# Moving the right operands of four matmul groups by 32 to 192 bytes, with pads in the on-chip memory

## The chip, the cores and the metric

The kernel runs on one core of a Trainium2 chip. The metric is the device time of one execution in microseconds (us), of which the median over several executions is taken. Lower is better.

## The reference

One decoder block for 512 tokens of width 1024, all in float32:

```
h = rmsnorm(x, pre_mix_norm)
q_r, k_r, v_r, g_r, q_s, k_s, v_s, gate_r, gate_s = split(h @ w_in)
y_r = (silu(g_r) * retention(q_r, k_r, v_r)) @ w_ret_out      # 4 heads, chunks of 128
y_s = sliding_window_attention(q_s, k_s, v_s, sinks) @ w_swa_out  # 8 heads, window 128
x = x + rmsnorm((sigmoid(gate_r) * y_r + sigmoid(gate_s) * y_s) @ w_out, post_mix_norm)
u = square(relu(rmsnorm(x, pre_mlp_norm) @ w_up))             # width 4096
out = x + rmsnorm(u @ w_down, post_mlp_norm)
```

## The kernel before

Every large product is made of three matmuls: each float32 operand is split in a high and a low part (`split`, lines 133 to 136: ScalarE casts the high part at L135, VectorE subtracts it at L136), and `mm3` (L176 to 181) adds high x high (L179), high x low (L180) and low x high (L181) in PSUM. A matmul holds one operand, the left one, still in the array (128 x 128, brought there by a weight load, PEld in the profile) and streams the other, the right one (256 or 512 columns), past it. TensorE (PE) loads the left operand of the next matmul while it streams the right one of the present matmul, so two reads of the on-chip memory run side by side.

The stages, in order of time, with the names that the profile gives to output, right and left operand:

- **Projections** (0 to 206 us): `ptok` (keys and values of the attention; right operand `wkv`, left `xg`), `pblk` (queries and keys; right `xg`, later `hT`; left `whi` and `wlo`, the split weights), `wide` (a fast matrix multiplication with seven products for v and g; here the weights stream, and `hT` and `hsum` are the left operands), with the attention and the retention between them.
- **Output of attention and gates** (206 to 354 us): `ys`, then eight calls of `wino_pair` (seven products of 256 columns instead of eight; right operands `hT` and the sums of its quarters `hsum`; left `whi`, `wlo` and the prepared sums `p24`, `p22`, which the profile calls `p`), between which `yr` (right `retT`) runs.
- **Mixing** (354 to 400 us): `ps` (left `mhi` and `mlo`, right `wo`).
- **Up projection** (400 to 557 us): `up` for three weight pairs (right `h2c`, `h2b`, `h2d`), then thirteen calls of `wino_pair` (right `h2c`, `h2d` and the sums `h2s`).
- **Down projection** (557 to 720 us): seven products with 512 columns, `p1` to `p7` (the profile calls them `p`), whose left operands are split from the activations `uc` by `left` (L1139) into the tiles `left0` and `left1`, and whose right operands are split from the weights (`raw`, `tch`). The last quarter runs in two halves of 256 columns, `p4c`.

Tiles lie in pools that are stacked one behind the other in each partition; when a pool is closed, later pools take its memory. A `pad` is a tile that nobody uses; it shifts what is allocated behind it:

```
def pad(pool, size, name="pad"):

    pool.tile([P, size // 4], F32, name=name, bufs=1)
```

All the tiles of a matmul are whole multiples of 256 bytes long, so that a tile's start modulo 256 is set by the pads ahead of it. The split weights `whi`, `wlo`, the sums `p24`, `p22`, and the tiles `xg`, `retT`, `swaT`, `mhi`, `wo` and `left` start at 128 modulo 256 in the built program. `hT`, `hsum`, `wkv`, `h2c`, `h2b`, `h2d` and `h2s` start at 64. The distance of this document is the start of the left operand less the start of the right one, modulo 256: 64 for `pblk` and `wino` with `hT` and `hsum`, for `ptok`, and for everything with `h2...`; 192 for `wide`; 0 for `ys`, `yr`, `ps`, `p`, `p4c`, the part of `pblk` with `xg`, and the products of the retention (`ret_st`, `ret_v`).

The order of the instructions is made by a scheduling layer: it places an instruction on its engine as soon as the tiles that it reads and writes allow, with priorities that the code gives (`high_priority`, `issue_after`). Where a new tile takes bytes of a closed pool's tile, the new tile's writer waits for the last reader of the old one. That matters between up and down projection: the pool `ring` with `left0` and `left1` (L1139) takes memory of `uctx`, which holds `h2c`, `h2d`, `h2s`, `p24`, `p22`. In the built program `h2s` ends at byte 141,888 of a partition, and the first `left0` begins at 141,952.

Of the kernel before, what the change touches and what calls it, by code (L numbers as in the profile page):

```python
# [94 lines left out]
def block_kernel(ctx, tc, x, xT, pre_mix, w_in, w_v, w_g, w_gate, w_ret, w_swa, w_out, sinks, post_mix,  # L95
# [13 lines left out]
    def pad(pool, size, name="pad"):  # L109

        pool.tile([P, size // 4], F32, name=name, bufs=1)
# [29 lines left out]
    def parts(src, shape):  # L141
        hi = stream.tile(shape, F32R, name="whi", tag="whi")
        lo = stream.tile(shape, F32R, name="wlo", tag="wlo")
        split(hi, lo, src)
        return hi, lo
# [149 lines left out]
    accpool = ctx.enter_context(tc.tile_pool(name="accpool", bufs=1))  # L295
    hctx = ExitStack()
    hpool = hctx.enter_context(tc.tile_pool(name="hpool", bufs=1))
    pad(hpool, 192)
    hT = [hpool.tile([P, KD, SEQ], F32R, name=f"hT{i}") for i in range(2)]
    hsum = [hpool.tile([P, 4, 4, 256], F32R, name=f"hsum{i}") for i in range(2)]  # L300


# [210 lines left out]
    def ret_keys(kT, h):  # L513

        ps = bank([P, NT - 1, P], "ret_k")
        for c in range(NT - 1):
            nc.tensor.transpose(ps[:, c, :], kT[:, c * P : (c + 1) * P], ident)
        kd = [rpool.tile([P, NT - 1, P], F32R, name=f"kd{i}", bufs=1) for i in range(2)]
        scale = chunk_sb[:, 0, h : h + 1]
        nc.scalar.mul(kd[0], ps, scale)  # L520
        nc.vector.scalar_tensor_tensor(
            kd[1], ps, scale, f(kd[0]), op0=ALU.mult, op1=ALU.subtract
        )
        return kd

    def ret_scores(qT, kT, h):
        ps = bank([P, NT, P], "ret_s")
        for c in range(NT):
            sl = slice(c * P, (c + 1) * P)
            nc.tensor.matmul(ps[:, c, :], kT[:, sl], qT[:, sl], start=True, stop=True)  # L530
        p = rpool.tile([P, NT, P], F32, name="pt", tag="qk")
        pt = [rpool.tile([P, NT, P], F32R, name=f"pt{i}", bufs=1) for i in range(2)]
        nc.vector.tensor_tensor(
            p, ps, decay_sb[:, h : h + 1, :].to_broadcast([P, NT, P]), op=ALU.mult
        )
        split(pt[0], pt[1], p)
        return pt
# [61 lines left out]
    def wide_sums(pool, w_, **kw):  # L599

        both = pool.tile([P, 2, 4, 512], F32, name="acc", **kw)
        sx, sy = both[:, 0], both[:, 1]
        nc.sync.dma_start(sx, w_[1, 0])
        nc.gpsimd.dma_start(sx, w_[1, 1], accum_op=ALU.add)
        nc.sync.dma_start(sy, w_[0, 0])
        return sx, sy
# [64 lines left out]
    def load_qk(h):  # L671
        return load_feature_blocks(w_in, (C_QR + h * RET_DK, C_KR + h * RET_DK))
# [67 lines left out]
    for h in range(RET_HEADS):  # L740
        if 0 < h < RET_HEADS - 1:
            wqk = load_qk(h + 1)
        v = parts(vg[:, :, h * RET_DV : (h + 1) * RET_DV], [P, NT, RET_DV])
        if h == RET_HEADS - 1:
            vg = vpool.tile([P, NT, D_MODEL], F32, name="vg", tag="vg")
            steps = wide(w_g, *wide_sums(xypool, w_g), vg)
            next(steps)
        kd = ret_keys(kT, h)
        pt = ret_scores(qT, kT, h)
        q_now = qc  # L750
        if h + 1 < RET_HEADS:
            qT = ret_block(wqk[0])
        else:
            next(steps)
        if h == 0:
            probs_t = swa_transpose(probs)
        states = ret_states(kd, v, h)
        if h == 0:
            swa_values(3, probs_t)

            bctx.close()
            gctx = ExitStack()
            wx = wino_pool(gctx)
            pad(wx, 64)
            xyctx = ExitStack()
            xypool = xyctx.enter_context(tc.tile_pool(name="xypool", bufs=1))
        if h + 1 < RET_HEADS:
            kT = ret_block(wqk[1])
        else:
            next(steps)  # L770
        ret_values(q_now, pt, states, v, h)
        if h + 1 < RET_HEADS:
            qc = [rpool.tile([P, SEQ - P], F32R, name=f"qc{i}", bufs=1) for i in range(2)]
            split(qc[0], qc[1], qT[:, P:])
# [226 lines left out]
    uctx = ExitStack()  # L1001
    h2pool = uctx.enter_context(tc.tile_pool(name="h2pool", bufs=1))
    h2spool = uctx.enter_context(tc.tile_pool(name="h2spool", bufs=1))
    pad(h2pool, 192)
    h2c = [h2pool.tile([P, 2, 4, 256], F32R, name=f"h2c{i}") for i in range(2)]
    h2d = [h2spool.tile([P, 4, 256], F32R, name=f"h2d{i}") for i in range(2)]
    h2s = [h2spool.tile([P, 4, 4, 256], F32R, name=f"h2s{i}") for i in range(2)]
    rspool = uctx.enter_context(tc.tile_pool(name="rspool", bufs=1))
    px = uctx.enter_context(tc.tile_pool(name="px", bufs=1))
    pad(px, 64)  # L1010
    wx = wino_pool(uctx)
    pctx = ExitStack()
    ppool = pctx.enter_context(tc.tile_pool(name="ppool", bufs=1))
    pad(ppool, 192)
    h2b = [ppool.tile([P, 4, 256], F32R, name=f"h2b{i}") for i in range(2)]
    quads = [
        [tuple(a[:, 0] for a in h2c), tuple(h2b)],
# [348 lines left out]
```

## Time and profile before

| | us |
|---|---|
| median of 3 runs | 724.63 (721.85 to 732.5) |
| span of the profiled execution | 719.9 |
| median less span | 4.7 |
| PE busy | 708.3 (98% of the span) |
| VectorE (DVE) busy | 535.8 (74%) |
| ScalarE (ACT) busy | 421.7 (59%) |
| GpSimd (POOL) busy | 60.3 (8%) |
| mean granted TensorE clock | 0.999 of full speed |

The span runs from the first to the last instruction of the one execution that was profiled; what lies around it is the difference to the runs' times. A matmul's duration holds a constant latency besides its streaming: matmuls of 256 columns that follow each other at 0.11 us each show 276 ns. So durations of different groups are compared among those of the same column count, and only what one has more than another costs time. In the view of one tile, a row gives the smallest, the median and the largest duration of a group, and when its first and last instruction started.

### The profile page before, as it was taken

What the parts mean: (1) busy time and instruction counts of PE and PEld (TensorE: products, weight loads), DVE (VectorE), ACT (ScalarE), POOL (GpSimd) and SP (SyncE); (2) the same over time, 40 slices, a digit from 0 to 9 for tenths busy, and PEclk for the clock granted to TensorE, in tenths of its full rate; (3) what the DMA queues carried; (4) which work ended last, traced back from release to release, by engine and by line L of the source; (5) the groups of instructions that cost most, each with busy time, mean ns of one, the idle gap of its engine ahead of it and who ended that gap; (6) DMA issues with size and microseconds to landing.
All of it is one profiled execution on the core that took longest, in us unless ns stands there. A gap on an engine that the chain in (4) does not pass through costs nothing.

```text
span 719.9 us, 11248 instructions
## 1 busy us (share of the span) xinstructions
PE 708.3 (98%) x4438; PEld 628.8 (87%) x4438; DVE 535.8 (74%) x808; ACT 421.7 (59%) x712; POOL 60.3 (8%) x75
## 2 busy tenths in 40 slices
PE   8999999999999999999999999999999999999996
PEld 7877878888888989989888999999999888888885
DVE  5699986667885667566845876877776788977797
ACT  6667676345665526344643776666668666655571
POOL 0200000201100000000002100000000110010010
PEclk9999999999999999999999999999999999999999
DMA  9964424916444455461563618777753999698603
GB/s 318 330 179 84 108 72 129 282 46 132 101 142 120 107 162 147 125 197 59 198 271 117 159 47 234 201 202 193 204 153 118 305 278 238 151 208 194 118 0 117
DMA packets 43605, 117.79 MB, mean 164 GB/s; under 512 B 3488, under 2 KB 21024, under 8 KB 37408
## 3 DMA queue, kind: packets, MB, share of 16 engines
q1 hardware_dynamic: 36784, 80.76, 31.8%
q0 software_dynamic: 6480, 36.18, 27.3%
q8 instruction: 35, 0.57, 0.3%
q14 instruction: 18, 0.15, 0.1%
q10 hardware_dynamic: 288, 0.14, 0.1%
HBM read 114.96 MB, written 2.10 MB: 163 GB/s over the span
## 4 chain that ended last, share of the span: by engine, by line
PE 79%; DVE 8%; DMA 5%; ACT 4%; issue 2%; POOL 0%; POOLq 0%; DVEq 0%; SPq 0%; ACTq 0%
PE wino L179 9%; PE wino L180 9%; PE wino L181 9%; PE p L181 5%; PE p L180 5%; PE p L179 5%; DVE wlo L136 3%; PE wide L179 3%; PE wide L180 3%; PE wide L181 3%; DMA raw<-in_w_in 3%; PE ps L180 2%; PE ps L181 2%; PE yr L181 2%; PE yr L180 2%; PE yr L179 2%
## 5 line engine op out<-in xcount | busy, mean ns | idle before, releaser
L136 DVE TENSOR_TENSOR wlo<-raw,whi 128x1024 fp32r<-128x1024 f32 x81 | 98.6, 1223 | 42.4 <-ACT whi L135 42.2
L135 ACT CAST whi<-raw 128x1024 fp32r<-128x1024 f32 x81 | 84.8, 1052 | 40.4 <-DMA raw<-in_w_down 7.6
L181 PE MATMUL p<-whi,left 128*128 128x512 f32 x216 | 84.1, 390 | 0.2 <-DVE left L136 0.2
L180 PE MATMUL p<-wlo,left 128*128 128x512 f32 x216 | 84.2, 390 | 0.0
L179 PE MATMUL p<-whi,left 128*128 128x512 f32 x216 | 84.0, 390 | 0.1
L181 PEld LDWEIGHTS p<-whi,left 128*128 128x128 f32 x216 | 40.5, 188 | 9.3 <-DVE left L136 1.0
L180 PEld LDWEIGHTS p<-wlo,left 128*128 128x128 f32 x216 | 40.5, 188 | 8.9 <-DVE wlo L136 0.4
L179 PEld LDWEIGHTS p<-whi,left 128*128 128x128 f32 x216 | 40.5, 188 | 8.7 <-ACT left L135 0.5
L136 DVE TENSOR_TENSOR wlo<-tch,whi 128x1024 fp32r<-128x1024 f32 x32 | 38.6, 1220 | 6.9 <-ACT whi L135 6.9
L135 ACT CAST left<-uc 128x1024 fp32r<-128x1024 f32 x28 | 29.3, 1050 | 23.4 <-PE p L180 23.4
L135 ACT CAST p<-rs 128x1024 fp32r<-128x1024 f32 x21 | 22.1, 1051 | 35.5 <-DVE rs L230 35.4
L136 DVE TENSOR_TENSOR left<-uc,left 128x1024 fp32r<-128x1024 f32 x28 | 34.1, 1221 | 10.4 <-ACT left L135 10.4
L135 ACT CAST whi<-tch 128x1024 fp32r<-128x1024 f32 x32 | 33.2, 1050 | 11.3 <-PE p L181 6.8
L136 DVE TENSOR_TENSOR p<-rs,p 128x1024 fp32r<-128x1024 f32 x21 | 25.7, 1226 | 15.4 <-ACT p L135 15.4
L136 DVE TENSOR_TENSOR wlo<-rs,whi 128x1024 fp32r<-128x1024 f32 x21 | 25.7, 1224 | 12.1 <-ACT whi L135 9.4
L136 DVE TENSOR_TENSOR wlo<-acc,whi 128x1024 fp32r<-128x1024 f32 x20 | 24.1, 1217 | 6.5 <-ACT whi L135 6.5
L179 PE MATMUL wino<-h2s,p 128*128 128x256 f32 x104 | 28.7, 276 | 0.0
L180 PE MATMUL wino<-h2s,p 128*128 128x256 f32 x104 | 28.7, 276 | 0.0
L181 PE MATMUL wino<-h2s,p 128*128 128x256 f32 x104 | 28.7, 276 | 0.0
L179 PE MATMUL wino<-h2c,whi 128*128 128x256 f32 x104 | 28.7, 276 | 0.0
L180 PE MATMUL wino<-h2c,whi 128*128 128x256 f32 x104 | 28.7, 276 | 0.0
L181 PE MATMUL wino<-h2c,wlo 128*128 128x256 f32 x104 | 28.7, 276 | 0.0
(354 smaller groups left out, 2317.7 us busy)
## 6 DMA issues: line engine op xcount, KB each, us to landing
tch<-in_w_down POOLq DMA_DIRECT2D x12, 1024.0 KB, 9.5
raw<-in_w_down SPq DMA_DIRECT2D x7, 1024.0 KB, 7.6
rs<-in_w_up SPq DMA_DIRECT2D x13, 512.0 KB, 4.2
rs<-in_w_up POOLq DMA_DIRECT2D x13, 512.0 KB, 5.7
raw<-in_w_up SPq DMA_DIRECT2D x13, 512.0 KB, 5.1
raw<-in_w_in SPq DMA_DIRECT2D x8, 512.0 KB, 5.2
acc<-in_w_v POOLq DMA_DIRECT2D x4, 1024.0 KB, 7.9
rs<-in_w_gate SPq DMA_DIRECT2D x8, 512.0 KB, 3.9
```

Source lines behind the costliest of these rows:

```text
L135: last["hi"] = nc.scalar.copy(hi, src)
L136: last["split"] = nc.vector.tensor_tensor(lo, src, f(hi), op=ALU.subtract)
L179: nc.tensor.matmul(ps, ah, bh, start=first, stop=False, skip_group_check=more)
L180: nc.tensor.matmul(ps, ah, bl, start=False, stop=False, skip_group_check=more)
L181: nc.tensor.matmul(ps, al, bh, start=False, stop=last, skip_group_check=more)
```

## The change

Six pads change their size or are new. No instruction is added or taken away. The diff in full:

```
-    pad(hpool, 192)
+    pad(hpool, 224)
     hT = [hpool.tile([P, KD, SEQ], F32R, name=f"hT{i}") for i in range(2)]
+    pad(hpool, 64, "pad2")
     hsum = [hpool.tile([P, 4, 4, 256], F32R, name=f"hsum{i}") for i in range(2)]
...
             wx = wino_pool(gctx)
-            pad(wx, 64)
+            pad(wx, 224)
             xyctx = ExitStack()
...
-    pad(h2pool, 192)
+    pad(h2pool, 160)
     h2c = [h2pool.tile([P, 2, 4, 256], F32R, name=f"h2c{i}") for i in range(2)]
+    pad(h2spool, 64, "pad2")
     h2d = [h2spool.tile([P, 4, 256], F32R, name=f"h2d{i}") for i in range(2)]
+    pad(h2spool, 160, "pad3")
     h2s = [h2spool.tile([P, 4, 4, 256], F32R, name=f"h2s{i}") for i in range(2)]
     rspool = uctx.enter_context(tc.tile_pool(name="rspool", bufs=1))
     px = uctx.enter_context(tc.tile_pool(name="px", bufs=1))
-    pad(px, 64)
+    pad(px, 128)
     wx = wino_pool(uctx)
     pctx = ExitStack()
     ppool = pctx.enter_context(tc.tile_pool(name="ppool", bufs=1))
-    pad(ppool, 192)
+    pad(ppool, 224)
     h2b = [ppool.tile([P, 4, 256], F32R, name=f"h2b{i}") for i in range(2)]
```

In the built program the tiles then start as follows (modulo 256), and the left operands `whi`, `wlo`, `p24`, `p22`, `xg` stay at 128:

| matmuls (count) | columns | moved tile | start before, now | distance before, now |
|---|---|---|---|---|
| `pblk` with `hT` (192) | 512 | `hT`, right | 64, 96 | 64, 32 |
| `wide` with `hsum` (192) | 512 | `hsum`, left | 64, 160 | 192, 32 |
| `wide` with `hT` (144) | 512 | `hT`, left | 64, 96 | 192, 224 |
| `wino` with `hT`, gates (288) | 256 | `hT`, right | 64, 96 | 64, 32 |
| `wino` with `hsum`, gates (384) | 256 | `hsum`, right | 64, 160 | 64, 224 |
| `ptok` (96) | 256 | `wkv`, right | 64, 160 | 64, 224 |
| `up` and `wino` with `h2c` (456) | 256 | `h2c`, right | 64, 32 | 64, 96 |
| `up` and `wino` with `h2d`, `h2b` (300) | 256 | `h2d`, `h2b`, right | 64, 96 | 64, 32 |
| `wino` with `h2s` (624) | 256 | `h2s`, right | 64, 0 | 64, 128 |

`h2s` now ends at byte 142,080, and the first `left0` still begins at 141,952: the two share 128 bytes. That moves instructions between up and down projection. On ScalarE at that place, before (in the rows, `left` is `left0`, `raw` and `tch` hold weights of the down projection, `uc` the activations):

```order
L276 COPY uc_3640<-wino 128x256
L135 CAST whi<-tch_4440 128x1024 x2
L135 CAST left_6073<-uc_3963 128x1024
L135 CAST left_6110<-uc_3963 128x1024
L135 CAST whi<-raw 128x1024 x2
L283 COPY uc_3640<-wino 128x256
L1112 ACTIVATE uc_3640<-wino 128x256
```

With the change:

```order
L276 COPY uc_3641<-wino 128x256
L135 CAST whi<-tch_4443 128x1024 x2
L135 CAST whi<-raw 128x1024
L283 COPY uc_3641<-wino 128x256
L135 CAST whi<-raw 128x1024
L135 CAST left_6076<-uc_3964 128x1024
L135 CAST left_6113<-uc_3964 128x1024
```

The two casts of `left0` have moved behind both casts of `raw`, and the first of them now waits for the last matmul of the last `wino_pair`. On PE at the same place, before (`p_6067` and `p_6068` are `p1`, `left_6073` is the first `left0` and `left_6074` the first `left1`, `p_5924` is `p22`):

```order
L179 MATMUL p_6067<-whi,left_6073 128x512
L180 MATMUL p_6067<-wlo,left_6073 128x512
L179 MATMUL p_6068<-whi,left_6073 128x512
L181 MATMUL p_6067<-whi,left_6074 128x512
...
L179 MATMUL p_6068<-whi,left_6073 128x512
L179 MATMUL wino<-h2s_3976,p_5924 128x256
L180 MATMUL wino<-h2s_3977,p_5924 128x256
...
L180 MATMUL p_6068<-wlo,left_6073 128x512
```

With the change (`p_6070` and `p_6071` are `p1`, `p_6072` and `p_6073` are `p2`):

```order
L181 MATMUL wino<-h2s_3979,p_5928 128x256
L179 MATMUL p_6070<-whi,left_6076 128x512
L180 MATMUL p_6070<-wlo,left_6076 128x512
L179 MATMUL p_6071<-whi,left_6076 128x512
L180 MATMUL p_6071<-wlo,left_6076 128x512
L179 MATMUL p_6072<-whi,left_6113 128x512
L180 MATMUL p_6072<-wlo,left_6113 128x512
L179 MATMUL p_6073<-whi,left_6113 128x512
L181 MATMUL p_6070<-whi,left_6077 128x512
```

Before, ten matmuls of `p1` stood ahead of the last product of the last `wino_pair` (twelve matmuls); now all twelve stand ahead of the first matmul of `p1`, and three of `p2` have moved up between those of `p1`. The load of the weights `tch1` (L1089 before) waits for the end of that last product in both programs.

More of the change, by code (lines that the diff above doesn't have):

```diff
@@ L297, in block_kernel @@
     hpool = hctx.enter_context(tc.tile_pool(name="hpool", bufs=1))
-    pad(hpool, 192)
+    pad(hpool, 224)
     hT = [hpool.tile([P, KD, SEQ], F32R, name=f"hT{i}") for i in range(2)]
+    pad(hpool, 64, "pad2")
     hsum = [hpool.tile([P, 4, 4, 256], F32R, name=f"hsum{i}") for i in range(2)]
@@ L763, in block_kernel @@
             wx = wino_pool(gctx)
-            pad(wx, 64)
+            pad(wx, 224)
             xyctx = ExitStack()
@@ L1003, in block_kernel @@
     h2spool = uctx.enter_context(tc.tile_pool(name="h2spool", bufs=1))
-    pad(h2pool, 192)
+    pad(h2pool, 160)
     h2c = [h2pool.tile([P, 2, 4, 256], F32R, name=f"h2c{i}") for i in range(2)]
+    pad(h2spool, 64, "pad2")
     h2d = [h2spool.tile([P, 4, 256], F32R, name=f"h2d{i}") for i in range(2)]
+    pad(h2spool, 160, "pad3")
     h2s = [h2spool.tile([P, 4, 4, 256], F32R, name=f"h2s{i}") for i in range(2)]
@@ L1009, in block_kernel @@
     px = uctx.enter_context(tc.tile_pool(name="px", bufs=1))
-    pad(px, 64)
+    pad(px, 128)
     wx = wino_pool(uctx)
@@ L1013, in block_kernel @@
     ppool = pctx.enter_context(tc.tile_pool(name="ppool", bufs=1))
-    pad(ppool, 192)
+    pad(ppool, 224)
     h2b = [ppool.tile([P, 4, 256], F32R, name=f"h2b{i}") for i in range(2)]
```

## The prediction

> **What bounds the kernel now.** I read the page first: busy times, granted clock, the chain that ended last.
>
> ```profile
> PE 708.3 (98%) x4438; PEld 628.8 (87%) x4438; DVE 535.8 (74%) x808; ACT 421.7 (59%) x712; POOL 60.3 (8%) x75
> PEclk9999999999999999999999999999999999999999
> PE 79%; DVE 8%; DMA 5%; ACT 4%; issue 2%; POOL 0%; POOLq 0%; DVEq 0%; SPq 0%; ACTq 0%
> ```
>
> PE is busy for 98% of the span, at full clock throughout, and holds 79% of the chain. The view of PE's waits, of which these are the longest and the last row of eight, sums to under 5 us:
>
> ```profile
> PE warm L336 <- POOL ident masks.py:199: 1.4, 1, 1.4
> PE p L181 <- DVE left L136: 0.2, 1, 0.2
> ```
>
> So the time is the number of matmuls by the spacing at which they follow each other. The change leaves the number alone and shifts where operands start; what it can do is change the spacing, or the waits. The next view asks whether spacing differs today among groups of equal shape: one tile's rows, smallest, median and largest duration, first the groups of 256 columns.
>
> ```profile
> L179 PE MATMUL ptok<-wkv,xg x32: 276/276/384, 6.0 to 17.0; 128*128 128x256 f32 x32
> L179 PE MATMUL ret_v<-st,qc x12: 283/283/287, 129.5 to 178.8; 128*128 128x256 f32 x12
> L180 PE MATMUL wino<-hT,whi x64: 276/281/283, 232.3 to 336.4; 128*128 128x256 f32 x64
> L180 PE MATMUL wino<-hsum,p x64: 276/281/281, 235.0 to 343.5; 128*128 128x256 f32 x64
> L179 PE MATMUL up<-h2c,whi x48: 276/281/281, 399.9 to 418.4; 128*128 128x256 f32 x48
> L179 PE MATMUL wino<-h2c,whi x104: 276/276/276, 435.0 to 551.6; 128*128 128x256 f32 x104
> L179 PE MATMUL wino<-h2s,p x104: 276/276/281, 437.7 to 561.2; 128*128 128x256 f32 x104
> L180 PE MATMUL p4c<-wlo,left x16: 280/283/283, 707.2 to 712.6; 128*128 128x256 f32 x16
> ```
>
> Three levels stand there. At distance 0 (`ret_v`, `p4c`) nearly all take 283 ns, 7 more than the floor of 276. At distance 64 there are two levels, 276 and 281: the up projection sits at 276, the gates mostly at 281. The groups of 512 columns:
>
> ```profile
> L179 PE MATMUL pblk<-hT,whi x64: 392/394/496, 42.0 to 160.1; 128*128 128x512 f32 x64
> L179 PE MATMUL pblk<-xg,whi x32: 389/389/501, 17.4 to 41.3; 128*128 128x512 f32 x32
> L181 PE MATMUL wide<-whi,hsum x64: 388/392/397, 61.3 to 201.1; 128*128 128x512 f32 x64
> L181 PE MATMUL wide<-whi,hT x48: 388/394/397, 55.8 to 206.6; 128*128 128x512 f32 x48
> L179 PE MATMUL yr<-retT,whi x64: 389/389/389, 251.7 to 353.9; 128*128 128x512 f32 x64
> L180 PE MATMUL p<-wlo,left x216: 388/389/498, 557.7 to 706.7; 128*128 128x512 f32 x108
> ```
>
> Here distance 0 (`yr`, `p`, `pblk` with `xg`) is the floor, 389, distance 64 (`pblk` with `hT`) takes 394, and 192 (`wide`) lies between, 388 to 397. So the distance goes with the spacing, but not alone: the same distance is good for one column count and bad for the other, and at 64 one group has both levels. The timeline of PE shows where the gates change from one to the other:
>
> ```profile
> 249.62 0.28 PE L180 MATMUL wino<-hsum,whi 128*128 128x256 f32 x1
> 249.73 0.28 PE L181 MATMUL wino<-hsum,wlo 128*128 128x256 f32 x1
> 250.23 0.39 PE L179 MATMUL wino<-hsum,p 128*128 128x256 f32 x1 [0.22 <-ACT sgs L283]
> 250.92 0.28 PE L181 MATMUL wino<-hsum,p 128*128 128x256 f32 x1
> 251.04 0.28 PE L179 MATMUL wino<-hsum,p 128*128 128x256 f32 x1
> 251.16 0.28 PE L180 MATMUL wino<-hsum,p 128*128 128x256 f32 x1
> ```
>
> Ahead of the wait they start every 0.11 us, behind it every 0.12. The view of `wino` for the next stretch of 168 matmuls, first and last row, has no other level any more:
>
> ```profile
> L179 PE MATMUL wino<-hT,whi x16: 281/281/281, 262.6 to 275.0; 128*128 128x256 f32 x16
> L181 PE MATMUL wino<-hsum,p x16: 281/281/281, 265.7 to 282.3; 128*128 128x256 f32 x16
> ```
>
> 167 steps in 19.7 us are 0.118 us each. A short wait thus set a phase between streaming and weight loads that lasted until the gates ended. My theory: the two reads meet in the same part of the memory when their distance, less their lag, falls in a window, and the meeting costs 5 to 7 ns per matmul. [...]
>
> **What could be gained at most.** With the floor of 276 and 389, the moved groups lose: `pblk` with `hT` 192 x 5 ns = 1.0 us; `wide` 336 x 3 (median about 392) = 1.0; the gates 672, three quarters of them at 281, so 672 x 3.8 = 2.6; `up` with `h2c` about half of 144 at 281 = 0.4. Together 5.0 us, 0.7% of the time. The groups that stay at distance 0 keep their 7 ns or nothing, since neither operand moves.
>
> **The terms by group.** No run before has the distances 32, 96, 128 or 224, so each is bounded by the nearest rows: for 256 columns 0 (+7 ns) and 64 (0 or +5), for 512 columns 0 (0), 64 (+5) and 192 (+3). Each term is the count by (chosen less present level); the ends stand in brackets.
>
> - `pblk` with `hT`, 32, between +0 and +5, middle 2.5: 192 x -2.5 ns = -0.5 us (-1.0 to 0).
> - `wide`, 32 and 224, between +0 and +5, middle 2.5, now 3: 336 x -0.5 = -0.2 (-1.0 to +0.7).
> - gates with `hT`, 32, between +0 and +7, middle 3.5, now 3.8: 288 x -0.3 = -0.1 (-1.1 to +0.9).
> - gates with `hsum`, 224: the same ends, as it lies as near to 0: 384 x -0.3 = -0.1 (-1.5 to +1.2).
> - `ptok`, 224, now at the floor: 96 x 3.5 = +0.3 (0 to +0.7).
> - `h2d` and `h2b`, 32, now at the floor: 300 x 3.5 = +1.0 (0 to +2.1).
> - `h2c`, 96: nearest to 64, so I keep its mix with a little on top, 1.0 after 0.8: +0.1 (-0.4 to +2.8).
> - `h2s`, 128: the farthest from 0, where the loss is largest, and 64 beside it is at the floor; I take 0.5 ns: 624 x 0.5 = +0.3 (0 to +4.3).
>
> Sum +0.8 us (-5.0 to +12.7).
>
> [...]
>
> **The moved instructions.** Between up and down projection `left0` now waits for the last reader of `h2s`. Before:
>
> ```profile
> 557.43 0.39 PE L179 MATMUL p<-whi,left 128*128 128x512 f32 x1
> 557.89 0.40 PE L179 MATMUL p<-whi,left 128*128 128x512 f32 x1
> 558.45 0.50 PE L181 MATMUL p<-whi,left 128*128 128x512 f32 x1 [0.16 <-DVE left L136]
> 558.79 0.40 PE L179 MATMUL p<-whi,left 128*128 128x512 f32 x1
> 561.45 0.28 PE L181 MATMUL wino<-h2s,p 128*128 128x256 f32 x1
> ...
> 556.67 1.04 ACT L135 CAST left<-uc 128x1024 fp32r<-128x1024 f32 x1
> 561.77 0.38 ACT L1112 ACTIVATE uc<-wino 128x256 f32<-128x256 f32 x1 [1.89 <-PE wino L181]
> 568.17 2.95 ACT L135 CAST whi<-tch 128x1024 fp32r<-128x1024 f32 x3 [2.29 <-DMA tch<-in_w_down]
> ...
> 570.18 0.39 PE L179 MATMUL p<-whi,left 128*128 128x512 f32 x1
> 570.53 0.19 PEld L180 LDWEIGHTS p<-wlo,left 128*128 128x128 f32 x1 [0.39 <-DVE wlo L136]
> 570.54 0.50 PE L180 MATMUL p<-wlo,left 128*128 128x512 f32 x1
> ```
>
> At a spacing of 0.23, PE lost 0.33 us from 557.89 to 558.45 and 0.11 to 558.79, on `left1`; and 0.13 from 570.18 to 570.54 with another 0.10 behind it, since the weights `tch1` came late. Together 0.67. With the change the twelve matmuls of the last product take the place of the first of `p1` at 557.43, and the next would start at 557.43 + 12 x 0.113 (the 0.118 of the slow gates less 5 ns) = 558.79. The last of them ends 0.28 after its start at 558.68, at 558.96; ScalarE follows 0.04 later (561.45 + 0.28 = 561.73 to 561.77), casts 1.04 and is done at 560.04; with some 0.15 to PE, `p1` starts at about 560.2: 1.4 lost. A new start costs 0.1 more (as at 558.79), and `p2` waits some 0.1 for the second cast: 1.6 in all. Behind the casts, ScalarE's work on `uc` for the third quarter waits, and nobody needs that within 10 us. The load of `tch1` is released at 558.96 in place of 561.73, so its cast comes some 2.8 earlier than 568.17, ahead of its use after 48 matmuls, and the 0.23 there is gone. Net 1.6 - 0.67 = +0.9; I take +1.0 (0 if other work fills the gap, +1.5 if VectorE delays `left1` once more).
>
> **The sum.** 719.9 + 0.8 + 1.0 = 721.7 us of span. The median of the runs lies 4.7 above the span of the profiled execution; kept, that gives 726.4.
>
> **The rivals.**
>
> 1. *All four distances clear the window.* For it: the present levels at 64 and 192 are not far from their floor, and 96 and 128 lie far from 0. Against it: 32 and 224 are the neighbours of 0, which costs 7 ns in every stretch of 256 columns. It would give back the 5.0: 719.9 - 5.0 + 1.0, with 4.7 on top 720.6.
> 2. *The up projection loses its floor: slower.* The place is 411 to 557 us, where today everything runs at 276. If `h2s`, `h2c`, `h2d` and `h2b` go to the 283 of distance 0, 1380 x 7 ns = 9.7 us, less the 0.4 that `h2c` loses now, with the gap of 1.0: 719.9 + 10.3 + 4.7 = 734.9. It decides once the median of `h2s` is above 279. For it: a change of phase by one wait took the gates from 276 to 281, and the up projection holds most of the moved matmuls. Against it: more than 1000 matmuls in a row held the floor.
> 3. *The distance is no cause, and the phase alone sets the level.* Then the pads do not do what they say: each stretch keeps the row it has, and only the moved instructions count: 719.9 + 1.0 + 4.7 = 725.6. For it: both levels at one distance. Against it: 283 at distance 0 in every stretch. [...]
>
> **How the numbers follow.** My forecast, 726.4, has a chance of 0.43, rival 1 0.21, rival 2 0.18, rival 3 0.15; 0.03 is left for levels that no row shows. The sum of the ends is 719.9 - 5.0 + 0 + 4.7 = 719.6 and 719.9 + 12.7 + 1.5 + 4.7 = 738.8. All ends of one sign together are unlikely above; I cut at rival 2 and give 719.5 to 735. About 2%, 14.5 us, is what a measurement of this kernel can tell from no change, since its own runs spread from 721.85 to 732.5. No case here reaches it: faster by over 2% 0.02, within 2% 0.94, slower by over 2% 0.04.
>
> **What would show it.** Right if `pblk` with `hT` falls below 394, `h2d` rises above 276, `h2s` stays within 2 ns of 276, and PE stands still for 1.2 to 1.8 us near the first `p1`. Rows of 276 and 389 everywhere would mean rival 1, a median of 280 or more on `h2s` rival 2, unchanged rows rival 3. A level above 283, or a wait that moves work outside of that one place, would make the working wrong.

## The result, and the profile after

| | before | changed |
|---|---|---|
| median of 18 runs each (us) | 727.02 (721.11 to 736.04) | 731.45 (730.57 to 732.34) |
| ratio of the two, 95% interval | | 1.0083 (1.0062 to 1.0103) |
| span of the profiled execution (us) | 719.9 | 729.9 |

The changed kernel is slower by 0.8%: a real difference, and within the 2% that count as no change. The number lies in the range, 5.0 above the forecast. What happened is not the likeliest case but the second rival: the up projection lost its floor. That rival left out the projections ahead of it, which lost 2 us more.

One thing about the runs of before has to be known to read every comparison below. They lie at two levels: of the 18, five lie between 721.1 and 721.9, nine between 726.3 and 728.5, one at 724.63; three above 732 are disturbed and count in no comparison. The changed kernel has one level, 1.8 us wide. So the change costs 10 us against the lower level, to which the profiled execution belongs (span 719.9), and 4 against the upper one, and the ratio mixes the two. What the two levels are is what experiments 7 to 11 ask.

The page of the changed kernel, total busy time and the engines' shares of the chain:

```profile
span 729.9 us, 11248 instructions
PE 718.0 (98%) x4438; PEld 638.3 (87%) x4438; DVE 535.3 (73%) x808; ACT 422.7 (58%) x712; POOL 63.7 (9%) x75
PE 87%; DVE 5%; DMA 3%; ACT 2%; issue 2%; POOL 0%; DVEq 0%; POOLq 0%; SPq 0%; ACTq 0%
```

The same 4438 records of matmuls take 718.0 us in place of 708.3: PE is as busy as before, and slower in what it does. The groups of 256 columns, in the order in which the prediction shows them (smallest, median, largest duration; first and last start):

```profile
L179 PE MATMUL ptok<-wkv,xg x32: 278/278/420, 6.0 to 19.0; 128*128 128x256 f32 x32
L179 PE MATMUL ret_v<-st,qc x12: 283/283/283, 129.4 to 178.8; 128*128 128x256 f32 x12
L180 PE MATMUL wino<-hT,whi x64: 277/280/285, 232.6 to 338.1; 128*128 128x256 f32 x64
L180 PE MATMUL wino<-hsum,p x64: 277/280/282, 235.5 to 345.2; 128*128 128x256 f32 x64
L179 PE MATMUL up<-h2c,whi x48: 277/281/284, 401.6 to 420.4; 128*128 128x256 f32 x48
L179 PE MATMUL wino<-h2c,whi x104: 277/281/283, 437.8 to 560.2; 128*128 128x256 f32 x104
L179 PE MATMUL wino<-h2s,p x104: 276/283/287, 440.6 to 567.3; 128*128 128x256 f32 x104
L179 PE MATMUL wino<-h2d,p x52: 278/281/285, 442.0 to 563.0; 128*128 128x256 f32 x52
L180 PE MATMUL p4c<-wlo,left x16: 282/283/283, 717.2 to 722.6; 128*128 128x256 f32 x16
```

From 400 us on, where `wino` with `h2c` stood at 276/276/276, no row of the up projection has its median under 280 any more, and most rows of `h2s` are at 283. The groups that did not move (`ret_v`, `p4c`) are where they were. The groups of 512 columns:

```profile
L179 PE MATMUL pblk<-hT,whi x64: 392/396/503, 42.9 to 160.0; 128*128 128x512 f32 x64
L179 PE MATMUL pblk<-xg,whi x32: 387/389/479, 19.3 to 42.3; 128*128 128x512 f32 x32
L181 PE MATMUL wide<-whi,hsum x64: 389/395/397, 62.1 to 201.4; 128*128 128x512 f32 x64
L179 PE MATMUL wide<-whi,hT x48: 392/396/508, 55.9 to 206.5; 128*128 128x512 f32 x48
L179 PE MATMUL yr<-retT,whi x64: 389/389/399, 252.8 to 355.6; 128*128 128x512 f32 x64
L180 PE MATMUL p<-wlo,left x216: 388/389/397, 569.3 to 716.7; 128*128 128x512 f32 x108
```

`pblk` at 32 is as bad as it was at 64. Of the 336 matmuls of `wide`, 99 took 390 ns or less before; 5 do now. The place between up and down projection, on PE and on ScalarE:

```profile
567.56 0.28 PE L181 MATMUL wino<-h2s,p 128*128 128x256 f32 x1
568.97 0.50 PE L179 MATMUL p<-whi,left 128*128 128x512 f32 x1 [1.14 <-ACT left L135]
569.31 0.39 PE L180 MATMUL p<-wlo,left 128*128 128x512 f32 x1
```

```profile
566.32 1.05 ACT L135 CAST whi<-raw 128x1024 fp32r<-128x1024 f32 x1 [0.69 <-PE wino L180]
567.87 1.99 ACT L135 CAST left<-uc 128x1024 fp32r<-128x1024 f32 x2 [0.50 <-PE wino L181]
```

From 567.56 to 568.97 are 1.41 us, 0.11 of which the matmul itself would take: 1.30 lost, for the reason that the prediction worked out and close to its size (1.4).

The sum can be made from the starts of the matmuls. From the start of one to the start of the next, the floor is 113.3 ns for 256 columns and 226.7 for 512 (in the profile of before, the steps of `wino` from 440 to 555 us and the usual steps of `p` from 600 to 700); what a matmul has above it (steps more than 15 ns above are waits and left out) is its group's loss:

| group (distance before, now) | mean loss before, ns | now, ns | change in the sum, us | term of the prediction |
|---|---|---|---|---|
| `pblk` with `hT` (64, 32) | 6.7 | 6.5 | 0.0 | -0.5 |
| `wide` (192; 32 and 224) | 2.6 | 6.5 | +1.3 | -0.2 |
| gates, `hT` and `hsum` (64; 32 and 224) | 3.4 | 4.9 and 3.5 | +0.4 | -0.2 |
| `ptok` (64, 224) | 0.0 | 4.4 | +0.3 | +0.3 |
| `h2d`, `h2b` (64, 32) | near 0 | 5.0 | +1.5 | +1.0 |
| `h2c` (64, 96) | 0.8 | 5.3 | +2.0 | +0.1 |
| `h2s` (64, 128) | 0.05 | 6.0 | +3.7 | +0.3 |

That is 9.2 of the 10.0 us by which the spans differ. The moved instructions are 1.0 more: 1.30 ahead of `p1`, 0.11 behind its first matmul and 0.2 at 580.3 us, where a `left` of VectorE comes late, together 1.64, less the 0.68 that `left1` and the late weights cost there before. Groups that were not moved add 0.2. Waits at the start, in the attention and in the gates differ by up to 1.5 us either way between the two profiles and sum to -0.4.

### The profile page after: what moved, and what is told of

Its sections match the earlier page's. It is cut to its first block, busy times and chain, and to the rows that moved or that the text cites. A ratio compares the mean times of both kernels' runs of the same rounds, so it can differ in the third digit from the quotient of the medians.

```text
span 729.9 us, 11248 instructions
## 1 busy us (share of the span) xinstructions
PE 718.0 (98%) x4438; PEld 638.3 (87%) x4438; DVE 535.3 (73%) x808; ACT 422.7 (58%) x712; POOL 63.7 (9%) x75
## 4 chain that ended last, share of the span: by engine, by line
PE 87%; DVE 5%; DMA 3%; ACT 2%; issue 2%; POOL 0%; DVEq 0%; POOLq 0%; SPq 0%; ACTq 0%
PE wino L179 8%; PE wino L180 8%; PE wino L181 8%; PE p L179 5%; PE p L181 5%; PE p L180 5%; PE wide L179 3%; PE wide L180 3%; PE wide L181 3%; PE pblk L179 3%; PE pblk L181 3%; PE pblk L180 3%; PE yr L179 2%; PE yr L180 2%; PE ps L179 2%; PE ps L180 2%
## 5 line engine op out<-in xcount | busy, mean ns | idle before, releaser
L179 PEld LDWEIGHTS p<-whi,left 128*128 128x128 f32 x216 | 40.5, 188 | 10.3 <-ACT left L135 2.0
L135 ACT CAST p<-rs 128x1024 fp32r<-128x1024 f32 x21 | 22.0, 1050 | 31.3 <-DVE rs L230 31.3
L181 PE MATMUL wino<-h2s,wlo 128*128 128x256 f32 x104 | 29.6, 284 | 0.0
L180 PE MATMUL wino<-h2s,whi 128*128 128x256 f32 x104 | 29.5, 284 | 0.0
L179 PE MATMUL wino<-h2s,whi 128*128 128x256 f32 x104 | 29.5, 284 | 0.0
L180 PE MATMUL wino<-h2s,p 128*128 128x256 f32 x104 | 29.4, 283 | 0.0
L179 PE MATMUL wino<-h2s,p 128*128 128x256 f32 x104 | 29.4, 283 | 0.0
L181 PE MATMUL wino<-h2s,p 128*128 128x256 f32 x104 | 29.3, 282 | 0.0
L179 PE MATMUL wino<-h2c,whi 128*128 128x256 f32 x104 | 29.2, 281 | 0.0
```

Of the source, the lines that this page charges most:

```text
L135: last["hi"] = nc.scalar.copy(hi, src)
L179: nc.tensor.matmul(ps, ah, bh, start=first, stop=False, skip_group_check=more)
L180: nc.tensor.matmul(ps, ah, bl, start=False, stop=False, skip_group_check=more)
L181: nc.tensor.matmul(ps, al, bh, start=False, stop=last, skip_group_check=more)
```

## The experiments

Three theories stood after the result. *Distance*: each group pays for its own distance, as in the table. *Order*: the loss comes from the moved instructions, which also move waits. *Phase*: a wait sets by lot whether a stretch of matmuls runs at its floor or above it, and the pads only changed the lot. Each experiment is the kernel before or the changed one with a short edit.

**1. The changed kernel with the old order.** The pool between `uctx` and the left operands gets 256 bytes more, so that `left0` no longer shares bytes with `h2s`; the distances stay those of the change.

```
-    pad(junks, 256)
+    pad(junks, 512)
```

> The changed kernel with 256 bytes more ahead of the left operands of the down projection, so that they no longer share bytes with h2s; all distances stay those of the change and p1 stands ahead of the last product again, as before. Theory 'distance' (the spacing is set by the distance of left and right operand): the median durations stay at 283 (h2s), 281 (h2c, h2d), 394 to 396 (pblk with hT, wide), the stall of 1.3 us ahead of the first p1 goes, span about 729, 1 us under the changed kernel's 729.9. Theory 'order' (the moved instructions are the loss): the up projection returns to 276 and the span to about 720.

Median 729.68 (10 runs), ratio to before 1.0068 (1.0041 to 1.0095), span 727.4. The wait ahead of `p1` is gone, the levels are not:

```profile
L179 PE MATMUL wino<-h2s,p x104: 276/282/287, 439.7 to 568.9; 128*128 128x256 f32 x104
```

`h2s` loses 6.0 ns per matmul, `h2c` 5.3, `h2d` 5.0, `pblk` and `wide` 6.5, as in the changed kernel. The order is worth 1.3 us by the starts of the matmuls there and 1.8 by the medians, and is not the cause of the rest.

**2. The projections alone.** The pads of `hpool` and of the first `wx` as in the change; `h2c`, `h2b`, `h2d`, `h2s` stay at 64.

```
-    pad(hpool, 192)
+    pad(hpool, 224)
...
+    pad(hpool, 64, "pad2")
...
-            pad(wx, 64)
+            pad(wx, 224)
```

> The kernel before with the new pads of hT and hsum alone; h2c, h2d, h2b, h2s stay at distance 64. Theory 'distance': pblk with hT and wide at 394 to 396, gates at 279 to 281, so up to 1.5 us more than before there; the up projection at 276 or at 281 throughout, by the phase that the last wait leaves (span about 721 or 727). Theory 'start' (an odd multiple of 32 bytes as start of any operand is slow): the same for these groups, and the up projection at 276.

Median 728.14, ratio 1.0031 (0.9995 to 1.0066), span 722.0. `pblk` and `wide` lose 6.5 ns, the gates 4.9 and 3.5, as in the changed kernel, and the up projection stands where it was before:

```profile
L181 PE MATMUL wide<-whi,hsum x64: 389/395/398, 62.2 to 202.5; 128*128 128x512 f32 x64
L179 PE MATMUL wino<-h2s,p x104: 276/276/279, 439.7 to 563.1; 128*128 128x256 f32 x104
```

So this part of the change is worth 2 us, and most of the loss lies behind 400 us. The runs of this kernel, in which only the up projection is still at 64, lie at two levels too: three at 723.3 to 723.8, seven from 727.5 up.

**3. The late `left0` alone.** The kernel before with 256 bytes more ahead of `h2c`: no distance changes, but all of `uctx` ends 256 bytes later.

```
-    pad(h2pool, 192)
+    pad(h2pool, 448)
```

> The kernel before with the pad ahead of h2c at 448 instead of 192 bytes: every distance stays at 64, but h2s now shares bytes with the first left operand of the down projection, so that p1 comes behind the last product as in the changed kernel. Theory 'distance': a stall of 1.3 us ahead of the first p1, 0.7 us of stalls there gone, so 0.5 to 1.0 us more than the kernel before at the same phase; up projection at 276 or 281. Theory 'order': about 729.

Median 726.24, ratio 1.0015 (0.9984 to 1.0046), span 724.8. This edit did more than it was meant to. By the built program's addresses the second tile of `h2c` (from byte 92,992) now shares bytes with `mhi` (at 100,992), so the start of the up projection waited as well. PE's waits show both:

```profile
PE p L179 <- ACT left L135: 1.1, 1, 1.1
PE up L179 <- DVE zg L984: 0.7, 1, 0.7
PE up L179 <- ACT h2c L135: 0.7, 1, 0.7
PE up L180 <- DVE h2c L136: 0.2, 1, 0.2
```

The wait ahead of `p1` costs the 1.3 us that it costs in the changed kernel. The median says nothing on it alone, since 2.5 us of waits at 400 to 403 are mixed in, and behind them matmuls start every 0.21 us, with a granted clock of 0.95 from 400 to 435 us, which costs another 1.4 (last section). `h2s` stayed at 276/276/276: the order of the changed kernel does not by itself make the up projection slow. All but one of the ten runs lie between 724.6 and 726.7: no second level.

**4. All starts moved, no distance changed.** Every tile behind `const` starts 32 bytes later.

```
-    pad(const, 192)
+    pad(const, 224)
...
-    pad(side, 96)
+    pad(side, 64)
```

> The kernel before with every tile of the stages shifted by 32 bytes (left operands start at 160, right ones at 96 modulo 256): all distances are those of before, all starts are odd multiples of 32. Theory 'distance': like the kernel before, 276 or 281 in the gates and in the up projection, 389 for yr and p, ratio to before about 1.00. Theory 'start': every group up to 283 or 396, some 4000 matmuls by 5 ns, span about 735 to 740.

Median 722.23, ratio 0.9981 (0.9945 to 1.0018), span 719.8. `pblk` loses 6.7 ns, `wide` 2.6, `wino` with `h2s` nothing, as before the shift. As far as a shift of both by 32 bytes can tell, it is the distance of the two operands and not where either lies. The runs lie at two levels like those of before: five of the nine at 721.7 to 722.2, four at 727.6 to 729.1, so the median is set by which level has one more. `ptok`, at distance 64 in both, ran at 276 in the profile of before and runs at 281 here:

```profile
L179 PE MATMUL ptok<-wkv,xg x32: 281/281/384, 5.9 to 17.3; 128*128 128x256 f32 x32
```

The gates, three quarters at 281 before, are at 281 from their first matmul. That is not the shift: the kernel before itself lost 0.0 ns on `ptok` in its first profile and 4.2 in the one of experiment 7. At distance 64 there are two phases, and which one a stretch gets changes from execution to execution.

**5 and 6. Other distances.** Both kernels are before with the larger `junks`; high and low parts of the `h2` tiles lie in one tile, so that their start can be set in steps of 8 bytes. In the first, `hT` and `hsum` go to 0, `h2d` and `h2b` to 48, `h2c` to 160, `h2s` to 192; in the second `h2s` goes to 48, `h2d` and `h2b` to 72, `h2c` to 80, and `hT` and `hsum` stay. The core of the first:

```
-    pad(hpool, 192)
+    pad(hpool, 256, "pad")
...
-    h2c = [h2pool.tile([P, 2, 4, 256], F32R, name=f"h2c{i}") for i in range(2)]
+    pad(h2pool, 96, "pad")
+    h2c = pair(h2pool, "h2c", (2, 4, 256), 0)
+    pad(h2spool, 96, "pad2")
+    h2d = pair(h2spool, "h2d", (4, 256), 16)
+    pad(h2spool, 96, "pad3")
+    h2s = pair(h2spool, "h2s", (4, 4, 256), 0)
```

> The kernel before with other starts: h2c at distance 160, h2s at 192, h2d and h2b at 48, hT and hsum at 0 (so pblk, wide, gates and ptok at 0); the left operands of the down projection keep off h2s. Theory 'distance' with what the runs so far gave (256 columns: 0 costs 6.5 ns, 32 5, 64 0 or 4.5, 96 5.3, 128 6, 224 3.5; 512 columns: 0 nothing, 32, 64 and 224 6.5): pblk and wide at 389 (2 us less), gates and ptok at 283, h2s between 3.5 and 6, h2c between 3.5 and 6, h2d between 0 and 5; span 725 to 729. If every distance but 64 cost the same, or the distance were no cause, pblk and wide would stay at 392 to 396.

> The kernel before with the up projection's right operands close to the good distance: h2c at 80, h2d and h2b at 72, h2s at 48; hT and hsum stay at 64. Theory 'distance' with a window around the bad distances whose edge lies near 64: on one side of 64 the level is 276 whatever the phase and the runs then lie at one level, about 721.5; on the other side it is 280 or more whatever the phase. A rival, that only multiples of 64 bytes are good: all three groups at 280 to 283, span 727 to 729.

Medians 729.76 and 729.92, ratios 1.0029 (0.9999 to 1.0058) and 1.0065 (1.0024 to 1.0105), spans 726.5 and 729.5; two runs of the second, at 733.1 and 739.0, lift its ratio. In the first, the 512-column groups are at their floor at distance 0, the gates at its 283, and `h2s` at 192 lies at 279:

```profile
L191 PE MATMUL pblk<-hT,whi x64: 389/389/499, 43.0 to 158.6; 128*128 128x512 f32 x64
L191 PE MATMUL wino<-hsum,p x64: 283/283/283, 233.3 to 343.4; 128*128 128x256 f32 x64
L191 PE MATMUL wino<-h2s,p x104: 277/279/282, 439.2 to 568.1; 128*128 128x256 f32 x104
```

In the second, `h2s` at 48 is at 282:

```profile
L191 PE MATMUL wino<-h2s,p x104: 278/282/287, 441.4 to 571.0; 128*128 128x256 f32 x104
```

`h2c` and `h2d` in the first lost more than I expected (up to 6 and 5), the other expectations of the first held; of the second, the window with an edge near 64 fell, and all three groups are at 280 or more. With what the others gave, the mean loss per matmul in ns by distance is (smallest and largest mean of a group in any run):

| distance | 0 | 32 | 48 | 64 | 72 | 80 | 96 | 128 | 160 | 192 | 224 |
|---|---|---|---|---|---|---|---|---|---|---|---|
| 256 columns | 5.3 to 6.7 | 4.8 to 5.2 | 5.3 to 6.4 | 0 or 4.45 | 6.6 to 6.9 | 5.9 to 6.0 | 4.4 to 5.4 | 5.5 to 6.1 | 6.5 to 6.6 | 4.5 | 3.3 to 4.5 |
| 512 columns | 0 to 1.3 | 6.4 to 6.5 | | 6.7 | | | | | | 2.5 to 2.8 | 6.6 |

Among the eleven distances tried, only 64 ever shows 256 columns at their floor, and it does so in one of its two phases (stretches that hold both lie between). The neighbours 48, 72 and 80 are about as bad as 0. Of the five distances that 512 columns had, only 0 is at the floor.

**7. A second profile of before.** The kernel before, unchanged.

> The kernel before once more, for its profile. If the two levels of its runs, about 721.5 and 727.5, are two phases of the up projection (1308 matmuls by 4.5 ns are 5.9 us), the profile shows either 276 throughout there and a span of about 720, or 281 and a span of about 726. A rival, something outside of the matmuls, would give 276 with a span of 726.

One run, 725.21, span 723.4. The up projection was at its floor again, so this profile did not show the upper level either. The 3.5 us more than in the first profile lie ahead of 57 us: behind the first matmul of the attention (`swa_s`, at 53.5 in the first and 57.1 in this) both spans have 666.4 and 666.3 left. PE's waits say where:

```profile
PE pblk L181 <- DVE wlo L136: 2.5, 1, 2.5
```

In the first profile that wait was 0.5. The chain behind that wait goes back to a load of weights that ScalarE casts at 31.3 us in the first profile and at 36.4 in this one. The other 1.5 us are a clock at 0.96 in the first 42 us (last section). So one profile can differ from the next by 3 us ahead of anything that the pads touch in the up projection.

**8. `h2s` alone.** Before with `h2s` at 128, everything else at 64, and the order kept.

```
+    pad(h2spool, 192, "pad3")
     h2s = [h2spool.tile([P, 4, 4, 256], F32R, name=f"h2s{i}") for i in range(2)]
...
-    pad(px, 64)
+    pad(px, 128)
...
-    pad(junks, 256)
+    pad(junks, 512)
```

> Kernel before with one group moved: h2s to distance 128, all others as before, and the pad of the ring behind the two left operands enlarged so that the order of the instructions stays that of before. Theory (each group pays its own distance): h2s about 6 ns per matmul over its floor, 624 of them, +3.7 us; h2c, h2d and h2b stay at 64 and at their floor; the span of a profiled execution is about 720.0 + 3.7 = 723.6. Theory on the two levels of the runs before (the up projection at distance 64 has two phases, 1308 matmuls by 4.45 ns = 5.8 us apart): with 624 of them moved away only 684 are left in the lottery, so the runs lie at two levels only 3.0 us apart, about 725 and 728. Rival (the two levels come from something else, such as the arrival of the first loads): they stay 5.8 apart, about 725 and 731. Rival (one moved group upsets its neighbours): h2c and h2d go to 281 too, and the span is 726.5 or more.

Median 726.64, ratio 1.0007 (0.9983 to 1.0031), span 724.7. `h2s` pays for its distance:

```profile
L179 PE MATMUL up<-h2c,whi x48: 280/281/282, 400.1 to 418.9; 128*128 128x256 f32 x48
L179 PE MATMUL wino<-h2c,whi x104: 275/276/282, 436.2 to 556.6; 128*128 128x256 f32 x104
L179 PE MATMUL wino<-h2s,p x104: 279/281/286, 439.1 to 566.2; 128*128 128x256 f32 x104
```

It loses 5.5 ns on 624 matmuls, 3.45 us. In this profile `up` is at 281 throughout, 4.45 ns on 286 matmuls, for the first time; the rest of `wino`, which now alternates with slow products, loses 1.2 on the average. What I expected of the runs, two levels 3 us apart, did not come: all twelve lie between 725.6 and 727.8. With slow products between them, the others do not stay in one phase for the whole stage, so the theory of two levels there was too simple.

**9. Setting the phase.** Before, with four transposes of the identity on PE, which nobody reads, between `up` and the first `wino_pair` of the up projection.

```
+    reset = bank([P, P], "reset")
+    for _ in range(4):
+        nc.tensor.transpose(reset, ident, ident)
     load_t(0)
     a = wino_first(up_weights(NH))
```

> Kernel before with four transposes of the identity on PE, read by nobody, ahead of the first product of the up projection's Winograd part; distances and all other instructions as before. In every profile so far the up projection at distance 64 went from 281 to 276 right behind such a row of transposes (at 410.56 in the kernel before). Theory (the phase is set where a stretch starts): the four cost about 0.5 us, behind them 1092 matmuls stand at 276 in every run, and the runs lose their upper level: one level at about 722, against 721.5 and 727.5 for the kernel before, a ratio of about 0.994. Rival (the phase is not set there, or falls as by lot): two levels as before, each 0.5 higher, ratio 1.000. Third case: the transposes set the phase to 281 in every run: one level at about 727.5.

Median 724.16, all twelve runs between 722.1 and 725.1, ratio to before 0.9974 (0.9947 to 1.0001), span 723.4. The upper level is gone. The median lies 2.7 us above the lower level of before, though, and 2 above what I expected: in the profile the transposes are 0.45 of that and `up` at 281 is 0.9, and the first matmul of `up` with `h2c` starts 2.0 us later (at 401.9 in place of 399.9), behind waits of 0.9 and 0.4 us for `mhi` and `mlo` that the first profile does not have, at a mean granted clock of 0.997 in place of 0.999. The profile also caught the switch. `up` runs at 281 from its first matmul to its last, and `wino`, with the same tiles at the same distance, at 276 behind the transposes:

```profile
L181 PE MATMUL up<-h2c,wlo x48: 280/281/282, 402.1 to 420.9; 128*128 128x256 f32 x48
L181 PE MATMUL wino<-h2c,wlo x104: 275/276/278, 438.6 to 555.3; 128*128 128x256 f32 x104
L179 PE MATMUL wino<-h2s,p x104: 275/276/280, 441.1 to 564.6; 128*128 128x256 f32 x104
```

```profile
437.72 0.28 PE L180 MATMUL up<-h2d,whi 128*128 128x256 f32 x1
437.84 0.28 PE L181 MATMUL up<-h2d,wlo 128*128 128x256 f32 x1
437.96 0.60 PE L1124 MATMUL reset<-ident 128*128 128x128 f32 x4
438.32 0.37 PE L179 MATMUL wino<-h2c,whi 128*128 128x256 f32 x1
438.52 0.28 PE L180 MATMUL wino<-h2c,whi 128*128 128x256 f32 x1
```

From 437.84 to 438.52 are 0.68 us in place of 0.23: the four cost 0.45. If the phase at 281 would have lasted, as it does in experiment 11, they return 4.45 ns on each of 1092 matmuls, 4.9 us, in those executions.

**10 and 11. The same at seven places.** Transposes ahead of every second product pair of the gates, ahead of the first and the fifth column of `up`, and ahead of `wino`; four at each place, or one.

```
+    def reset(ps):
+        for _ in range(4):
+            nc.tensor.transpose(ps, ident, ident)
...
+        if fresh:
+            reset(chain[:, :P])
         product(chain, "11", "11")
```

> Kernel before with four transposes of the identity at seven places where a stretch of 256 columns begins: ahead of the first, third, fifth and seventh product pair of the gates (each of the last three follows a stretch of 512 columns), ahead of the first and of the fifth column of the up projection, and ahead of its Winograd part. Distances as before. Theory (at distance 64 the entry sets the phase, and an entry from transposes that did not wait sets the floor): gates, up and wino stand at 276 throughout; the gates give back 672 x 3.4 ns = 2.3 us, the first part of the up projection up to 1.2, each place costs 0.45, 3.2 in all. One level of runs at 721.5 to 724, median about 722.5, ratio 0.993. Rival (the entry into the gates goes by another rule): the gates stay at 281 behind the transposes, the runs lie about 2 higher, at 725.

> As the version with four transposes at seven places, with one in place of four. Theory (the change of shape at the entry is what counts): the same rows, each place at about 0.15 us, 1.0 in all, median about 720.5, ratio 0.990. Rival (it takes a row of transposes that run at their own pace of 109 ns): one sets nothing, gates at 281 behind the stretches of 512 columns, and two levels of runs as before, about 722 and 728.

With four: median 727.33, ratio 1.0011 (0.9988 to 1.0034), 12 of 13 runs between 726.0 and 729.0 and the profiled one at 731.95. With one: 729.22, ratio 1.0039 (1.0017 to 1.0061), all twelve runs between 728.5 and 729.9. Both theories of an entry that sets the floor fell. With four, `wino` of the up projection is at 276, but it came to that level already inside `up`, behind the row of transposes `tin`; the four ahead of `up` had left it at 281. The three gate stretches that follow `yr` stayed at 281 too, here the second of them, and PE's waits on ScalarE for `sgs` rose from 0.2 to 1.7 us:

```profile
L179 PE MATMUL wino<-hT,whi x8: 281/281/363, 299.0 to 301.6; 128*128 128x256 f32 x8
```

So only experiment 9 shows four transposes turning 281 into 276. One set two of those three gate stretches to 276:

```profile
L179 PE MATMUL wino<-hT,whi x16: 276/276/367, 263.4 to 275.4; 128*128 128x256 f32 x16
...
L179 PE MATMUL wino<-hT,whi x16: 281/281/364, 294.0 to 306.4; 128*128 128x256 f32 x16
...
L179 PE MATMUL wino<-hT,whi x16: 276/276/367, 324.8 to 336.8; 128*128 128x256 f32 x16
```

and left the whole up projection behind 410 us at 281:

```profile
L179 PE MATMUL wino<-h2c,whi x104: 281/281/363, 436.3 to 557.6; 128*128 128x256 f32 x104
L179 PE MATMUL wino<-h2s,p x104: 276/281/281, 439.2 to 567.2; 128*128 128x256 f32 x104
```

This is a profile with the up projection at 281 and no distance changed. `wino` loses 4.41 ns on 1092 matmuls and `up` 3.4 on 286, 5.8 us, against 0.4 in the first profile of before. The two levels of before lie about 6 apart (medians of the two clusters 721.4 and 727.6), so this phase is most likely the upper one; no profile of before itself fell on it. Which entry gives which phase I could not work out: the same row of transposes (`tin`) inside `up`, with the same short wait, led to 276 in the first profile and to 281 in that of experiment 9.

**12. Setting the phase in the changed kernel.** Experiment 1 with the four transposes at the seven places.

> The changed kernel with the enlarged pad of the ring (order at the first product of the down projection as before) and four transposes at the same seven places. Theory (distances of 32, 96 and 128 have no floor to be set): gates at about 118 ns from start to start, up and wino at 118 to 119, as without the transposes; the seven places cost 3.2 us, median 729.7 + 3.2 = 732.9. Rival (the distances only make the bad phase likelier, and a fresh entry sets the floor there too): gates, up and wino at 276, about 11 us less, median about 722.

Four runs, median 734.91, ratio 1.0125 (1.0085 to 1.0164), span 732.5, 2.0 above what I expected; the profile has 1.1 us of new waits in the down projection. Nothing went to a floor:

```profile
L179 PE MATMUL wino<-hT,whi x64: 277/280/366, 232.6 to 339.1; 128*128 128x256 f32 x64
L179 PE MATMUL wino<-h2s,p x104: 274/283/287, 442.9 to 572.3; 128*128 128x256 f32 x104
```

In `wino`, `h2s` loses 6.1 ns, `h2c` 5.4, `h2d` 5.0. A fresh entry that reaches the floor at 64 does not reach it at 32, 96, 128 or 224. That tells the distance from the phase: of these distances only 64 has a phase that reaches the floor, and the changed kernel has taken its matmuls out of the draw.

## Why the prediction was right and wrong

- **The number.** The time lies inside the range, and it is slower, as forecast. But the upper end of the range is the time of rival 2, so lying in it says little for the likeliest case, which had +0.8 us for the spacing, where 9.2 came. Of its four signs two came: `h2d` rose above 276, and PE stood still for 1.3 us at the first `p1`. `pblk` did not fall below 394 (396), and `h2s` did not stay within 2 ns of 276 (283).
- **What bounds the kernel, and by what the change can act.** Right. The number of matmuls stayed, and the spacing moved 9.2 of 10.0 us.
- **`h2s`, `h2c`: the step that failed.** The prediction priced 128 at 0.5 ns because "64 beside it is at the floor", and let `h2c` keep its mix at 96. It measured 6.0 and 5.3 ns, 3.7 and 2.0 us in place of 0.3 and 0.1. It had seen both phases at 64, and still took the floor of one stretch for the price of the distance and carried it to the neighbours. The rows of one distance with two levels gave no level to carry. Distance 0, where every stretch of 256 columns showed 7 ns, was the better neighbour for all of them.
- **The middles.** `h2d` and `h2b` at 32 were put at 3.5 ns and measured 5.0; `ptok` and the gates with `hsum` at 224 at 3.5, measured 4.4 and 3.5; the gates with `hT` at 3.5, measured 4.9. Here the way of pricing held within 1.5 ns. For 512 columns the middle of 2.5 was too low, and so was the end of +5, which came from medians of durations (394 less 389): from start to start `pblk` lost 6.7 already before. 6.5 at 32 and 6.6 at 224 meant that `wide` lost 1.3 us and `pblk` gave nothing back.
- **The moved instructions.** Right: 1.30 against 1.4 at the place, 1.64 against 1.6 in all, 1.0 net against 0.9. In one detail it came otherwise: the late weights no longer cost their 0.23, but a `left` of VectorE at 580.3 us cost 0.2 instead.
- **From span to median.** The 4.7 us that were carried over from the first three runs were a second failed step. The time of the run that was profiled is 1.76 above its span (731.66 against 729.9). The rest of the 4.7 was the difference between an execution at the lower level and a median of three between the two. Rival 2's time of 734.9 was too high by 3.5, 2.9 of it by this term.
- **The rivals.** The second one happened in the up projection, at the point that was named: the median of `h2s` went to 283, above 279. That its span of 719.9 + 10.3 = 730.2 is within 0.3 of the 729.9 measured is luck: it put 9.3 on the up projection, at 7 ns each, and nothing on the projections, where 7.2 and 2.0 were measured. What was set against it, that more than 1000 matmuls in a row had held the floor, was true of one phase of one distance. The first rival fell at every distance. The third, that the phase alone sets the level, fell for the distances moved to: in experiment 8 `h2s` at 128 lost 5.5 ns beside neighbours at 64 that lost 1.2, and in experiment 12 no entry brought the floor back. It is half true of the distance moved from: at 64 the phase is worth 5.8 us by experiment 11.
- **The theory of the two reads.** That the two run at once is in the trace of before: at 249.51 us a weight load of 0.19 us starts together with a matmul of 0.28. That they meet in one part of the memory, in a window, at a lag, is still my reading. The rows show 276 against 283 for the same matmuls of `h2s` with the same instructions, moved by pads alone, and not a place in the chip. No lag told the levels apart either: ahead of the wait at 250 us (step 0.113) as behind it (0.118), a load starts within 0.01 us of a matmul.

The experiments lead to one version with a lower median than both: the kernel before with four transposes ahead of `wino` (experiment 9), 724.16 against 727.29 for the kernel before in the same comparison. Its interval just reaches 1.000, so against before the gain of 0.3% is likely and not certain; against the changed kernel it is about 1%.

## What to carry to other kernels

Where PE is busy all the time and does not wait, compare the durations of matmuls of one shape across groups: the start of the streamed operand against that of the loaded one was worth 3 to 7 ns of 113 here, and pads decide it without touching an instruction. Before a row is taken as the price of a layout, see whether that layout shows one level everywhere, or two; a level that came by lot cannot be carried to a neighbour, nor counted on in the next execution. And compare runs as distributions: two clusters before and one after were worth more here than the medians.

## What the runs showed of the hardware

- In these runs the spacing of float32r matmuls went with the distance of the two operands, 113.3 to 120.2 ns from start to start for 256 columns, and a shift of both by 32 bytes changed nothing (experiment 4: `pblk` 6.7, `wide` 2.6 and `h2s` 0 ns above the floor, as before). That I count it modulo 256 rests on the kernel before: by its addresses `h2s` lies 64 and 576 bytes (modulo 1,024) from `p`, 320 and 832 from `whi`, and all six of its rows have a median of 276. Of the eleven distances tried, 256 columns ran at 113.3 ns only at 64, and there in one of two phases, 113.3 or 117.8, that held over more than 1000 matmuls (experiments 9 and 11); of five, 512 columns ran at 226.7 only at 0. So none of the starts tried for `hT` serves `pblk` and the gates at once.
- Behind the wait ahead of `ptok`, some executions run 17 matmuls at half speed, 0.21 us from start to start, and others none. The changed kernel shows it, with a granted clock of 0.50 from 7.9 to 11.0 us and 0.96 over the first 42; experiment 7 has 0.96 there too, and the profile of before, with 1.00, does not show it:

```profile
7.67 0.28 PE L180 MATMUL ptok<-wkv,xg 128*128 128x256 f32 x1
7.79 0.37 PE L181 MATMUL ptok<-wkv,xg 128*128 128x256 f32 x1
7.96 0.42 PE L179 MATMUL ptok<-wkv,xg 128*128 128x256 f32 x1
8.17 0.42 PE L180 MATMUL ptok<-wkv,xg 128*128 128x256 f32 x1
```

  In the changed kernel it costs 1.6 us, and lasts from 7.8 to 11.2. Experiment 3 shows the same behind its waits ahead of `up`: steps of 0.21 us from 403.67 on, and a clock of 0.95 from 400 to 435 us. What brings it on, the runs do not show. In the 3.4 us ahead of the drop PE was busy for 1.92 us in the changed kernel (4.41 to 7.82) and for about 1.8 in experiment 3 (400.0 to 403.4). In the profile of before, whose clock stayed at 1.00, it was busy for 2.13 us from 4.78 to 8.19 us.
